# Another order of the seven products of a down projection, other places for the weight sums, and two PSUM tiles for the last two token tiles

## The chip, the cores and the metric

The kernel runs on one core of a Trainium2 chip. The metric is the device time of one execution in microseconds (us); several runs are timed and their median is given. The profile shows one execution, recorded by the hardware profiler. TensorE (PE in the profile) multiplies matrices into PSUM, ScalarE (ACT) and VectorE (DVE) do elementwise work, GpSimd (POOL) here subtracts halves of weights and issues some transfers, SyncE (SP) issues most loads.

## The reference, cut to what matters

One layer of a streaming encoder on 512 tokens and 16 learned meta tokens, d_model 1024, everything in float32. Two mixers (stick-breaking attention and gated linear attention) are merged by gates, projected, normalised and added to the residual. Then the gated MLP follows, with a causal depthwise convolution over tokens, d_ff 2816:

```python
hn = _rmsnorm(h, norm_ffn_pre[l])
up = hn @ w_ffn_up[l]
act = jax.nn.gelu(_causal_dwconv(up, conv_w[l], conv_b[l]), approximate=True)
ffn = (act * (hn @ w_ffn_gate[l])) @ w_ffn_down[l]
h = h + _rmsnorm(ffn, norm_ffn_post[l])
```

The change lies in `@ w_ffn_down` and in the normalisation of its result.

## The kernel before

**Precision.** Every float32 factor is split into a high part, rounded to the format fp32r that TensorE takes (`act.copy`, line 135), and a low part, the difference (`dve.tensor_tensor` subtract, line 136). A product is three matmuls: high by high, high by low, low by high. `split` (lines 134 to 136) does it with one instruction on ScalarE and one on VectorE.

**The down projection by seven products.** The activation A (tokens by d_ff) is cut into 2 x 2 blocks, two halves of the tokens by two halves of d_ff, and so is the weight B (d_ff by d_model). A scheme of the Strassen and Winograd kind computes the four result blocks with seven block products in place of eight. The sums of A blocks (S1 to S4) are made on VectorE at the end of the up/gate loop (lines 963 to 968); those of B blocks are made in place in one buffer `tw`, which first holds B11:

- t1: `tw += B12` (loaded into a small buffer, `raw_t`),
- t2: `tw += B22` (which lies in `tv`),
- t4: `tw += B21` (loaded into `raw_t`), with its signs arranged in the A sums.

`add` (line 1035) issues one such sum on VectorE (line 1039). The buffer `tv` first holds B22; an accumulating transfer issued by GpSimd (`by_transfer`, line 1046) then adds B12 onto it.

The products, with their A operand, B operand and PSUM accumulator: p1 (A11, B11, qa), p5 (S1, tw after t1, qd), p6 (S2, tw after t2, qb), p3 (S4, tv, qd), p7 (S3, tv after the transfer, qb), p4 (A22, tw after t4, qe), p2 (A12, B21 loaded again, qa). The profile names the accumulators dA, dD, dB, dE. p3 adds to what p5 left in qd, p7 to what p6 left in qb, p2 to what p1 left in qa. In between, p1's, p5's and p6's values are read out: a copy of qa on ScalarE (line 1076), a copy of qd on ScalarE (line 1084) and an addition from qb on VectorE (line 1089).

**Chunks.** `product` (lines 996 to 1019) walks d_ff in six chunks (`CH`, line 977: five of two slices of 128, one of one). A chunk splits its weight rows into `wh` and `wl` (128 x 1024), gets the A operand, and gives 12 matmuls of 512 columns (6 in the last). A11 and S1 are split beforehand (`whole`); for the other five products `late_split` (line 1024) splits the A chunk here, into `sh` and `sl` (128 x 512). The last two chunks are issued together, sorted by token tile (line 1015), so the first token tile is complete half of 18 matmuls before the second. `beside` is called once per chunk, after its splits: that is where the sums are put.

**Buffers.** `wh` and `wl` have two buffers in each of two pools, used two chunks in turn; `sh` and `sl` have two; `raw` has three. `tv` lies in the place of A11 and `hbr` (the residual, read back for the end) in the place of S1, so their loads wait for p1's and p5's matmuls. PSUM has eight banks of 128 x 512 float32: `mmt` (line 68) gives a tile of two banks, `pst` (line 71) a tile of one; two of each tag ("mm", "s", "z") exist. Line 1048's `halves` cuts a two-bank tile into its two token tiles.

**What sets the order.** The text of the kernel gives dependencies and priorities: the framework simulates the engines with its own costs when it builds the program, and puts on each engine, at each moment, the earliest-written instruction that is ready in the simulation. An instruction that is written late can so come early. On the chip each engine then keeps this fixed order, and waits where an input is late. Matmuls are ordered in the same way.

**The end.** For each of four token tiles of 128 rows, `square` sums squares on ScalarE (line 1052), `gain` multiplies by the norm's gain on VectorE (line 1055), `finish` (line 1057) forms the reciprocal root from the sums (line 1060 and lines 119 to 131), scales and adds the residual (line 1064, two instructions) and issues two output writes (line 1065). The first two token tiles end with p2.

## Time and profile before

| | |
|---|---|
| median of three runs | 975.08 us (972.68 to 976.45) |
| the profiled execution's own time | 973.69 us |
| its span (first to last instruction) | 972.0 us |
| mean granted TensorE clock | 0.987 |
| TensorE matmul busy | 941.1 us, 97% |
| VectorE busy | 661.6 us, 68% |
| ScalarE busy | 488.8 us, 50% |
| first and last matmul of the down projection start | 851.72 and 961.84 us |

Rows of groups give line, engine, operation, output and inputs with shapes, count, busy time and mean duration. Rows of a timeline give start, duration, engine, line and operation, and in brackets the idle time of the engine before it and what ended that. Where several instructions are merged (x2), the duration runs from the first start to the last end; neighbouring instructions of an engine can overlap a little. A row of windows gives the stretch, its length, then the busy time and count for PE, PEld (weight loads), DVE, ACT and POOL, the granted clock, the DMA engines' share and GB/s.

### The profile page before, as it was taken

Reading aid. Unit: us, or ns where it says so; the run is one execution under the profiler, and the core shown is the slowest. Engines: PE = TensorE matmul, PEld = TensorE weight load, DVE = VectorE, ACT = ScalarE, POOL = GpSimd, SP = SyncE. Lnnn points to the kernel's source line nnn. Section 1 sums busy time; section 2 is a strip of 40 time slices with the busy share of each in tenths; the row PEclk is TensorE's granted clock in tenths of the full one; section 3 lists DMA queues with packets and bytes.
Section 4 is the critical chain, followed back from the end, with each engine's and each line's share of the span. In section 5 each row is a group of like instructions: output and inputs, shape, how many; then the busy total and the mean of one; then the engine's idle time right before and its main releaser. Section 6 shows DMA issues by size and latency. Waiting matters only on the chain.

```text
span 972.0 us, 16625 instructions
## 1 busy us (share of the span) xinstructions
PE 941.1 (97%) x6588; PEld 867.5 (89%) x6588; DVE 661.6 (68%) x1110; ACT 488.8 (50%) x913; POOL 356.6 (37%) x268
## 2 busy tenths in 40 slices
PE   7999999999999998999999899999999999999995
PEld 7999999999999998999998679999999999887874
DVE  6675867767547877777859968555455445489877
ACT  5664645546367565675754245433333333344663
POOL 6523232222234554444545352444444444100200
PEclk9999999999999999999999899999999999999998
DMA  7122212221222221232213363232333332278712
GB/s 215 45 66 66 66 49 62 66 66 45 66 66 66 84 70 45 65 88 61 71 55 96 118 222 119 68 107 88 99 97 87 89 108 87 87 270 296 159 36 105
DMA packets 129727, 92.79 MB, mean 95 GB/s; under 512 B 4064, under 2 KB 114914, under 8 KB 129650
## 3 DMA queue, kind: packets, MB, share of 16 engines
q1 hardware_dynamic: 126178, 82.55, 28.8%
q10 hardware_dynamic: 1968, 6.29, 1.7%
q0 software_dynamic: 1504, 2.88, 1.6%
q8 instruction: 52, 0.85, 0.4%
q14 instruction: 25, 0.20, 0.1%
HBM read 87.52 MB, written 4.19 MB: 94 GB/s over the span
## 4 chain that ended last, share of the span: by engine, by line
PE 80%; DVE 12%; issue 3%; ACT 2%; POOL 2%; DMA 1%; DVEq 0%; POOLq 0%; ACTq 0%
PE pt_up L110 13%; PE ga L956 13%; PE pt_gr L110 5%; PE pt_gv L110 5%; PE pt_mg L110 4%; PE pt_go L110 4%; PE dA L1018 3%; PE pt_gk L110 2%; PE pt_sv L110 2%; PE pt_ms L110 2%; PE wo L890 2%; PE pt_gq L110 2%; PE dD L1018 2%; PE pt_sk L110 2%; PE dB L1018 2%
## 5 line engine op out<-in xcount | busy, mean ns | idle before, releaser
L90 POOL TENSOR_TENSOR wl_up<-raw_up,wh_up 128x1024 fp32r<-128x1024 f32 x22 | 53.0, 2410 | 67.6 <-ACT wh_up L89 67.6
L90 POOL TENSOR_TENSOR wl_ga<-raw_ga,wh_ga 128x1024 fp32r<-128x1024 f32 x22 | 55.2, 2510 | 56.6 <-ACT wh_ga L89 56.6
L110 PE MATMUL pt_up<-h2l,wh_up 128*128 128x256 f32 (+1 forms) x352 | 73.6, 283 | 0.3 <-DVE h2l L205 0.2
L110 PE MATMUL pt_up<-h2h,wh_up 128*128 128x256 f32 (+1 forms) x352 | 73.6, 283 | 0.2 <-ACT h2h L204 0.2
L110 PE MATMUL pt_up<-h2h,wl_up 128*128 128x256 f32 (+1 forms) x352 | 73.2, 282 | 0.0
L956 PE MATMUL ga<-h2h,wl_ga 128*128 128x512 f32 (+1 forms) x192 | 72.2, 376 | 0.0
L956 PE MATMUL ga<-h2l,wh_ga 128*128 128x512 f32 (+1 forms) x192 | 72.2, 376 | 0.0
L956 PE MATMUL ga<-h2h,wh_ga 128*128 128x512 f32 (+1 forms) x192 | 72.0, 375 | 0.0
L89 ACT CAST wh_up<-raw_up 128x1024 fp32r<-128x1024 f32 x22 | 23.0, 1049 | 85.4 <-PE pt_up L110 76.2
L110 PEld LDWEIGHTS pt_up<-h2h,wh_up 128*128 128x128 f32 x352 | 56.9, 189 | 2.2 <-ACT h2h L204 0.5
L110 PEld LDWEIGHTS pt_up<-h2l,wh_up 128*128 128x128 f32 x352 | 55.5, 189 | 0.7 <-DVE h2l L205 0.7
L110 PEld LDWEIGHTS pt_up<-h2h,wl_up 128*128 128x128 f32 x352 | 55.4, 189 | 0.0
L956 PEld LDWEIGHTS ga<-h2h,wl_ga 128*128 128x128 f32 x192 | 36.2, 189 | 7.0
L947 DVE SCALAR_TENSOR_TENSOR cy<-pt_up,cw,cy 128x511 f32<-128x511 f32 (+1 forms) x22 | 16.4, 745 | 37.7 <-ACT cy L944 37.7
L956 PEld LDWEIGHTS ga<-h2l,wh_ga 128*128 128x128 f32 x192 | 36.2, 188 | 6.2
L956 PEld LDWEIGHTS ga<-h2h,wh_ga 128*128 128x128 f32 x192 | 36.2, 188 | 6.1
L947 DVE SCALAR_TENSOR_TENSOR yp<-pt_up,cw,yp 128x511 f32<-128x511 f32 (+1 forms) x22 | 16.4, 745 | 30.9 <-ACT yp L944 30.9
L89 ACT CAST wh_ga<-raw_ga 128x1024 fp32r<-128x1024 f32 x22 | 23.0, 1048 | 25.2 <-PE ga L956 24.7
L135 ACT CAST sh_p<-As 128x512 fp32r<-128x512 f32 (+1 forms) x30 | 17.4, 583 | 30.7 <-PE dB L1018 11.5
L1046 POOL DMA_DIRECT2D tv<-in_w_ffn_down_dram x6 | 7.1, 1184 | 69.2 <-DVE wl_p L136 69.2
L90 POOL TENSOR_TENSOR wl_gr<-raw_gr,wh_gr 128x1024 fp32r<-128x1024 f32 x8 | 19.0, 2370 | 35.9 <-ACT wh_gr L89 33.1
L90 POOL TENSOR_TENSOR wl_gv<-raw_gv,wh_gv 128x1024 fp32r<-128x1024 f32 x7 | 16.9, 2418 | 38.2 <-ACT wh_gv L89 38.2
(558 smaller groups left out, 3265.6 us busy)
## 6 DMA issues: line engine op xcount, KB each, us to landing
raw_up<-in_w_ffn_up_dram SPq DMA_DIRECT2D x22, 512.0 KB, 3.9
raw_ga<-in_w_ffn_gate_dram SPq DMA_DIRECT2D x22, 512.0 KB, 3.8
raw_t<-in_w_ffn_down_dram SPq DMA_DIRECT2D x10, 512.0 KB, 6.7
raw_gv<-in_w_in_dram SPq DMA_DIRECT2D x8, 512.0 KB, 3.8
raw_gr<-in_w_in_dram SPq DMA_DIRECT2D x8, 512.0 KB, 3.9
raw_mg<-in_w_in_dram SPq DMA_DIRECT2D x8, 512.0 KB, 3.8
raw_go<-in_w_gla_out_dram SPq DMA_DIRECT2D x8, 512.0 KB, 4.1
raw_ms<-in_w_in_dram SPq DMA_DIRECT2D x8, 512.0 KB, 3.9
```

What stands on the lines that cost most here:

```text
L89: act.copy(hi_out, raw)
L90: lo_eng.tensor_tensor(out=lo_out, in0=raw, in1=f32(hi_out), op=ALU.subtract)
L110: pe.matmul(dst, a[:, k, :], b[:, k, lo:hi], start=n == 0, stop=n == len(steps) - 1)
L135: act.copy(hi, src)
L890: pe.matmul(d0[i], m[k][:, t], w, start=k == 0 and q == 0, stop=k == 7 and q == 2)
L947: dve.scalar_tensor_tensor(out=y[:, d:], in0=pt[:, : SEQ - d], scalar=c, in1=y[:, d:], op0=ALU.mult, op1=ALU.add)
L956: pe.matmul(pg_[:, lo:hi], a[:, k, :], b[:, k, lo:hi], start=lo == 0 and k == 0 and q == 0, stop=k == KT - 1 and q == 2, skip_group_check= ...
L1018: pe.matmul(dsts[i], a, b, start=first and k == 0 and edge[0], stop=last and k == NP - 1 and edge[1], skip_group_check=True)
L1046: return lambda n, q, nk: pool.dma_start(out=t[:, q : q + nk, :], in_=block(s, c, q, nk), accum_op=ALU.add)
```

## The change

The products are issued in the order p1, p5, p3, p6, p7, p4, p2, where p6 stood before p3. The t2 sums are no longer the source of p6: three of them are issued beside p5's chunks 3 to 5 and three beside p3's chunks 0 to 2 (`t2(-3)` and `t2(3)`). The t4 sums stand beside p6 and p7 instead of p3 and p7, every second chunk each. The accumulating transfers onto `tv` are issued beside p6's chunks instead of p3's. The addition from qb (old line 1089) moves into the loop behind p6, ahead of the subtraction, the square and the gain that used to follow p3.

The PSUM tiles change places: qa, the accumulator of p1 and p2, becomes two tiles of one bank (dA0 and dA1); qd, which was two such tiles, becomes one tile of two banks (dD). qb stays one tile of two banks. The loads of `tv` are written ahead of the copies of qa.

```diff
-        qa = halves(mmt("dA"))
-        product("p1", whole(A11), lambda q, nk: first.get(q, tw[:, q : q + nk, :]), qa, True, True,
-                lambda n, q, nk: add(plain(0, R, "t1"), "t1", q, nk))
+        def t2(shift):
+            def of(n, q, nk):
+                if 0 <= n + shift < len(CH):
+                    add(kept(tv), "t2", *CH[n + shift])
+            return of
+        def t4(odd):
+            def of(n, q, nk):
+                if n % 2 == odd:
+                    add(plain(1, L, "t4"), "t4", q, nk)
+            return of
+        qa = [pst("dA0"), pst("dA1", "z")]
+        product("p1", whole(A11), lambda q, nk: first.get(q, tw[:, q : q + nk, :]), qa, True, True, t1)
...
-        qd = [pst("dD0"), pst("dD1", "z")]
-        product("p5", whole(S1), kept(tw), qd, True, True)
+        qd = halves(mmt("dD"))
+        product("p5", whole(S1), kept(tw), qd, True, True, t2(-3))
         for i in range(2):
             act.copy(yb[:, 2 + i, R], qd[i])
+        product("p3", late_split(S4), kept(tv), qd, False, True, t2(3))
         qb = halves(mmt("dB"))
-        product("p6", late_split(S2), lambda q, nk: add(kept(tv), "t2", q, nk), qb, True, True)
+        product("p6", late_split(S2), kept(tw), qb, True, True, later(by_transfer(tv, 0, R), t4(0)))
         for i in range(2):
             dve.tensor_tensor(out=yb[:, i, R], in0=qb[i], in1=p1[:, i, :], op=ALU.add)
-        tv_sum = by_transfer(tv, 0, R)
-        product("p3", late_split(S4), kept(tv), qd, False, True, half_t4(0))
-        for i in range(2):
             dve.tensor_tensor(out=yb[:, i, R], in0=qd[i], in1=yb[:, i, R], op=ALU.subtract)
             square(i, yb[:, i, R], 1)
             gain(i, yb[:, i, R], R)
-        tv_sum = lambda n, q, nk: None
-        product("p7", late_split(S3), kept(tv), qb, False, True, half_t4(1))
+        product("p7", late_split(S3), kept(tv), qb, False, True, t4(1))
```

`later` calls its jobs one after the other for a chunk; `t1` is the old sum beside p1 under a name.

## The prediction

> **What bounds the kernel now.** I read the page first, then the stages of the down projection, then its waits, then the timelines of single engines around each gap. The page's first rows:

> ```profile
> span 972.0 us, 16625 instructions
> PE 941.1 (97%) x6588; PEld 867.5 (89%) x6588; DVE 661.6 (68%) x1110; ACT 488.8 (50%) x913; POOL 356.6 (37%) x268
> ```

> TensorE sets the pace, and the diff touches only what follows the first matmul of the down projection:

> ```profile
> 851.72 0.40 PE L1018 MATMUL dA<-wh_p,A 128*128 128x512 f32 x1
> ```

> From 851.72 to the end are 120 us. What can be won there is TensorE's idle time and the stretch behind its last matmul; the matmuls themselves, 462, stay. Three of the stages, and the waits of the second one:

> ```profile
> 882.20:897.70 15.50, 13.78 (x57) 10.07 (x55) 15.50 (x18) 7.70 (x12) 1.11 (x1) 1.00 0.78 268
> 900.40:915.50 15.10, 15.10 (x67) 12.21 (x67) 11.76 (x16) 9.19 (x13) 5.13 (x5) 1.00 1.11 227
> 930.80:946.70 15.90, 15.55 (x68) 12.40 (x68) 14.18 (x20) 10.73 (x17) 0.00 (x0) 1.00 0.15 37
> ...
> PEld dB L1018 <- DVE sl_p L136: 3.4, 4, 1.4
> PE dB L1018 <- DVE sl_p L136: 1.8, 3, 0.9
> ```

> The columns are window, length, then busy time (count) of PE, PEld, DVE, ACT, POOL. The first row is product p6 (into dB): VectorE busy 15.50 of 15.50, and only 57 matmuls, where p3 in the next row has 67 in 15.10 with VectorE at 11.76. TensorE waits there for `sl`, the low half of the split A operand. The gaps one by one (start, duration):

> ```profile
> 888.01 0.40 PE L1018 MATMUL dB<-wl_p,sh_p 128*128 128x512 f32 x1
> 888.84 0.50 PE L1018 MATMUL dB<-wh_p,sl_p 128*128 128x512 f32 x1 [0.43 <-DVE sl_p L136]
> 889.17 0.39 PE L1018 MATMUL dB<-wh_p,sh_p 128*128 128x512 f32 x1
> ...
> 894.34 0.40 PE L1018 MATMUL dB<-wl_p,sh_p 128*128 128x512 f32 x1
> 895.19 0.50 PE L1018 MATMUL dB<-wh_p,sl_p 128*128 128x512 f32 x1 [0.45 <-DVE sl_p L136]
> ...
> 896.46 0.40 PE L1018 MATMUL dB<-wl_p,sh_p 128*128 128x512 f32 x1
> 897.79 0.50 PE L1018 MATMUL dB<-wh_p,sl_p 128*128 128x512 f32 x1 [0.94 <-DVE sl_p L136]
> ...
> 934.26 0.39 PE L1018 MATMUL dE<-wl_p,sh_p 128*128 128x512 f32 x1
> 935.00 0.73 PE L1018 MATMUL dE<-wh_p,sl_p 128*128 128x512 f32 x2 [0.35 <-DVE sl_p L136]
> ```

> Matmuls overlap, so I count from start to start. The undisturbed pace is 0.232 (959.75 to 961.84, below, are nine steps). The steps into the waiting matmuls are 0.83, 0.85 and 1.33, which lose 0.60 + 0.62 + 1.10 = 2.3 us; each restart costs another 0.1 (888.84 to 889.17 is 0.33), four of them in p6, so p6 loses about 2.7 us. At p7 to p4 934.26 to 935.00 loses 0.5 more, 0.6 with its restart. The other products run through. So some 3.5 us lie in the middle, and after the last matmul (ends 962.24) the span runs on for 9.8 us.

> **The change part by part.** (1) The t2 sums (tw += tv) leave p6, whose source they were, and stand in p5 and p3, three each; the t4 sums (tw += raw_t) must now follow p6's own splits of tw, so they move from p3/p7 to p6/p7. Where did they run before?

> ```profile
> 892.18 2.35 DVE L1039 TENSOR_TENSOR tw<-tw,raw_t 128x1024 f32<-128x1024 f32 x2
> 896.19 1.22 DVE L1039 TENSOR_TENSOR tw<-tw,raw_t 128x1024 f32<-128x1024 f32 x1
> L1039 DVE TENSOR_TENSOR tw<-tw,raw_t x12: 683/1218/1224, 858.2 to 897.7; 128x1024 f32<-128x1024 f32 x10, 128x512 f32<-128x512 f32 x2
> L1039 DVE TENSOR_TENSOR tw<-tw,tv x6: 684/1218/1226, 875.5 to 885.2; 128x1024 f32<-128x1024 f32 x5, 128x512 f32<-128x512 f32 x1
> ```

> Though written into p3 and p7, the last t4 sum ran at 897.7, still inside p6: the scheduler pulls a sum forward as soon as its inputs allow. The 896.19 one directly holds up the `sl` that ends the 1.33 step. Pitch of such an operation is 2.35 - 1.22 = 1.13, so six sums (five whole, one half) are 6.3 us. After the change p6 holds four of its own weight splits that buffers do not let run earlier (3 x 1.13 + 0.6 = 4.0), four `sl` (2.2), two weight splits of p7 (2.3) and five or six t4 sums (5.7 to 6.3): 14.2 to 14.8 in 15.3, 93 to 97%. That lies between the 100% that lost 2.7 us and the 78% (11.76 of 15.10) that lost nothing; p4 at 89% lost 0.6. I take 0.8 lost in p6 (bounds 0 and 3.2, the old 2.7 and another 0.5 as in p4): **-1.9**, bounds -2.7 to +0.5. The t2 sums cost nothing: they stay limited by tv's landing (the first at 875.5), and p5 and p3 have the room (11.76 of 15.10). If that cover is gone, each is 1.13. What moves with them on the queues:

> ```profile
> raw_t<-in_w_ffn_down_dram SPq DMA_DIRECT2D x10, 512.0 KB, 6.7
> ...
> DMA to landing us min/median/max: 9.0/10.0/10.7
> ```

> The raw_t loads of t4 keep their order on SyncE (three raw buffers, 6.7 us to landing) and are wanted later than before, so they are there. The six accumulating tv transfers (the second row, L1046, alone on GpSimd's queue) need p3's splits of tv and t2's reads of it; p3 now runs a whole product (15.3) ahead of p6, so they start earlier and their 10 us are over before p7. I book nothing for either; a p7 that waits for a transfer would show at its first chunks.

> (2) Product order p1 p5 p6 p3 p7 p4 p2 becomes p1 p5 p3 p6 p7 p4 p2. Before, p5 and p3 (both into dD) had p6 between them, and p6 and p7 (both into dB) had p3. Now they are neighbours, and each first result must be read out before the next product adds to it. **p5 to p3**: ScalarE copies dD.

> ```profile
> 881.95 0.39 PE L1018 MATMUL dD<-wh_p,S 128*128 128x512 f32 x1
> 882.18 0.40 PE L1018 MATMUL dB<-wh_p,sh_p 128*128 128x512 f32 x1
> ...
> 882.25 1.06 ACT L1084 COPY yb<-dD 128x512 f32<-128x512 f32 x2
> ```

> TensorE went on at 882.18 because p6 followed. Now p5's end (882.34) releases both copies, 1.06, and TensorE resumes at about 882.36 + 1.06 + 0.03 = 883.45 instead of 882.18: **+1.3**. Bounds: 0.1 when each half is guarded alone, 2.3 when a 1.06 cast stands ahead on ScalarE. Other matmuls can't fill it: the buffers of sh and sl (two each) belong to p3's first chunks. **p6 to p7**: VectorE adds p1 to dB (L1089). The nearest rows are the same addition at p7 to p4:

> ```profile
> 930.56 0.40 PE L1018 MATMUL dB<-wh_p,sl_p 128*128 128x512 f32 x1
> 930.80 0.43 PE L1018 MATMUL dE<-wh_p,sh_p 128*128 128x512 f32 x1
> ...
> 931.32 1.28 DVE L1111 TENSOR_TENSOR yb<-dB,p 128x512 f32<-128x512 f32 x2
> ```

> An `sl` stood ahead of it, so the pair ended at 932.60, and a next product into dB would have resumed at 932.65 instead of 930.80: **+1.85**. Bounds 0.2 (halves guarded alone) and 3.0 (one more 1.13 operation ahead). Behind it on VectorE then stand p7's `sl` and the two subtractions L1103; p7 has both its first `sl` buffers filled by then, and I book nothing more.

> [...]

> (3) dA becomes two tiles, dA0 and dA1. p2's last matmuls are sorted by token tile, so tile 0 ends nine matmuls early:

> ```profile
> 959.75 0.39 PE L1018 MATMUL dA<-wh_p,sl_p 128*128 128x512 f32 x1
> ...
> 961.84 0.40 PE L1018 MATMUL dA<-wh_p,sl_p 128*128 128x512 f32 x1
> ...
> 962.27 0.60 ACT L1052 ACTIVATE dj<-dA 128x512 f32<-128x512 f32 x1 [4.02 <-PE dA L1018]
> 963.78 0.60 ACT L1052 ACTIVATE dj<-dA 128x512 f32<-128x512 f32 x1
> ...
> 964.57 1.40 DVE L1064 SCALAR_TENSOR_TENSOR yb<-yb,a_out,hbr 128x512 f32<-128x512 f32 x2
> 965.89 0.68 DVE L1055 TENSOR_TENSOR yb<-dA,g3bc 128x512 f32<-128x512 f32 x1
> 967.25 1.41 DVE L1064 SCALAR_TENSOR_TENSOR yb<-yb,a_out,hbr 128x512 f32<-128x512 f32 x2
> ```

> Tile 0 was complete at 960.14, yet its square began at 962.27, with ScalarE idle for 4.02: the wait goes by the whole tile. With two tiles everything of tile 0 moves up by 2.1, its final pair from about 964.4 to 962.3, ending 963.7. Tile 1's square then starts at 962.27 instead of 963.78, its sum at 963.65 behind that pair, its gain multiply at 963.70 instead of 965.89: 2.2 earlier, and the rest follows at the old distances (965.89 to the end of the last row, 968.66, is 2.77): it ends at 966.5, **-2.1** with a little taken off for the order of the small operations. Bounds: -2.8 (tile 1 runs as undisturbed as tile 0 did, 962.27 to 964.4 + 1.41) and -0.2. The output writes keep their distance.

> This also says that the prices of (2) go by the whole tile, since dD and dB are each one tile of two banks after the change.

> **Sum**: -1.9 + 1.3 + 1.85 - 2.1 = -0.85. The profiled execution took 973.69 (span 972.0 and 1.69 around it) and would take 972.8; the median of the runs, 975.08, is 1.4 above it, so I say 974.2.

> **The rivals.** (A) The halves of dD and dB are guarded bank by bank. Half 0 of a product is complete nine matmuls (2.1 us) before half 1, so its read-out is hidden, and the first matmuls of the next product cover the second: +0.3 in place of 3.15, sum -3.7, time 971.4. Against it stands the 962.27 row; for it only that a half is a bank. 17%. [...]

> (B) Slower: VectorE stays full in p6. If the scheduler pulls all six t4 sums into p6, with more than 15.3 us of work there (a seventh 1.13 operation decides), `sl` comes late as before, p6 keeps its 2.7, and L1089 starts behind a further sum: 3.0. Sum 0 + 1.3 + 3.0 - 2.1 = +2.2, time 977.3. For it: the 892.18 and 896.19 rows. Against: t2 is gone from there. 17%.

> (C) The split of dA buys little, because the scheduler places tile 0's last matmul next to tile 1's. It has done so where the tiles are separate already:

> ```profile
> 946.20 0.62 PE L1018 MATMUL dE<-wh_p,sl_p 128*128 128x512 f32 x2
> ...
> 946.63 1.29 DVE L1122 TENSOR_TENSOR yb<-dE,yb 128x512 f32<-128x512 f32 x2
> ```

> Two `sl` matmuls end p4 together and both tiles are read after 946.6. In p2 the 959.75 row stands in its sorted place, which speaks against it. Then -0.3 in (3): sum +0.95, time 976.0. 11%.

> **How the numbers follow.** Forecast 55%, A 17%, B 17%, C 11%. A measurement of this kernel tells 0.5% (4.9 us) from no change: under 970.2 is faster, over 980.0 slower. A crosses that only with (1) near its end of -2.7 and (3) near -2.8, a third of its chance, and scatter adds a little: 7%. B crosses with p6 at 3.2 and both read-outs at their upper ends, a quarter: with scatter 6%. The rest, 87%, is no difference. The range, 971.0 to 977.9, takes in A's and B's values and leaves out their far ends, about 2 in 10. The forecast's own range is 972.4 to 976.2.

> **What would show it.** In the changed profile: p6's `sl` waits of TensorE below 1 us in total (step 1; above 2 us is B); a TensorE wait for ScalarE's copies of dD at the start of p3 and one for VectorE's additions from dB at the start of p7, 1.3 and 1.85 (none is A); a square of dA0 starting about 2.1 us ahead of the last matmul's end, and 7.7 instead of 9.8 us from there to the end of the span (step 3; C if not). The prediction is wrong if the end of the last matmul moves by more than 3 us either way, or if an earlier product gets a stall that it did not have.

## The result, and the profile after

| | before | after |
|---|---|---|
| median, us | 974.42 (971.74 to 976.69, six runs) | 981.19 (979.11 to 982.05, six runs) |
| ratio to before | | 1.0065 (95%: 1.0043 to 1.0088) |
| the profiled execution's own time, us | 973.69 | 982.05 |
| its span, us | 972.0 | 980.3 |
| first start to last end of the down projection's matmuls, us | 851.72 to 962.24 | 852.50 to 971.13 |
| from there to the end of the span, us | 9.8 | 9.2 |

The change made the kernel slower by 0.65%, where 974.2 and "no difference" had been forecast. The profiled execution of after is the slowest of its six. The page of after begins:

```profile
span 980.3 us, 16625 instructions
PE 944.9 (96%) x6588; PEld 871.2 (89%) x6588; DVE 662.2 (68%) x1110; ACT 488.7 (50%) x913; POOL 357.1 (36%) x268
```

The work is the same, and so is every engine's busy time, but for 3.8 us more on TensorE (941.1 before). Some 2.9 of them lie in the two half-clock stretches below (an estimate: 6.76 us of busy time for 17 matmuls that take 3.9 at the pace of 0.23). The down projection's matmuls take 118.6 us instead of 110.5, 8.1 more; another 0.8 lies ahead of them, where the diff touches nothing, and the stretch behind them is 0.6 shorter. The chain of waits of after (start, duration, what) shows the places:

```profile
882.46 0.70 ACT wh_p L135
...
883.42 1.07 ACT yb L1105 x2
...
897.08 8.30 DMA raw_t<-in_w_ffn_down_dram
...
921.56 1.29 DVE yb L1113 x2
```

Three links that are not TensorE's account for what is new: the copies of dD (p5 to p3), a load of 8.30 us in the middle of p6, and the additions from dB (p6 to p7). The second was in no part of the forecast. TensorE's timeline of after at the three places:

```profile
882.72 0.39 PE L1018 MATMUL dD<-wh_p,S 128*128 128x512 f32 x1
884.53 0.50 PE L1018 MATMUL dD<-wh_p,sh_p 128*128 128x512 f32 x1 [1.43 <-ACT yb L1105]
...
903.23 0.39 PE L1018 MATMUL dB<-wl_p,sh_p 128*128 128x512 f32 x1
907.36 0.79 PE L1018 MATMUL dB<-wh_p,sl_p 128*128 128x512 f32 x1 [3.74 <-DVE sl_p L136]
...
920.78 0.39 PE L1018 MATMUL dB<-wh_p,sl_p 128*128 128x512 f32 x1
922.99 0.47 PE L1018 MATMUL dB<-wh_p,sh_p 128*128 128x512 f32 x1 [1.83 <-DVE yb L1113]
...
924.92 0.63 PE L1018 MATMUL dB<-wl_p,sh_p 128*128 128x512 f32 x1
925.35 0.63 PE L1018 MATMUL dB<-wh_p,sl_p 128*128 128x512 f32 x1
```

Counted from start to start against a pace of 0.23, the three steps are 1.81, 4.13 and 2.21 us and lose 1.6, 3.9 and 2.0. Behind the last two the matmuls do not go on at 0.23 but at 0.43 (924.92 to 925.35). The windows of after (window, length, then busy time and count of PE, PEld, DVE, ACT and POOL, the granted clock, the DMA share, GB/s) say why:

```profile
907.30:910.71 3.41, 3.35 (x8) 2.68 (x9) 3.41 (x5) 0.00 (x0) 0.00 (x0) 0.50 0.73 190
924.40:927.81 3.41, 3.41 (x9) 2.69 (x9) 3.35 (x6) 1.61 (x4) 0.00 (x0) 0.50 0.00 0
927.60:939.80 12.20, 12.20 (x54) 9.82 (x53) 7.40 (x10) 6.28 (x11) 0.00 (x0) 0.99 0.01 1
```

The granted clock is 0.50 for 3.41 us behind each of the two gaps, and only 8 or 9 matmuls pass there; later it is 0.99. Each such stretch costs some 1.5 us, an estimate (3.41 us less 8 or 9 steps of 0.23 is 1.6 or 1.3).

Why did the load come so late? VectorE's queue in p6, the transfers that GpSimd issued just before, and the loads of the t4 sums on SyncE's queue, all of after:

```profile
895.82 1.23 DVE L1039 TENSOR_TENSOR tw<-tw,raw_t 128x1024 f32<-128x1024 f32 x1
...
900.77 1.23 DVE L136 TENSOR_TENSOR wl_p<-tw,wh_p 128x1024 fp32r<-128x1024 f32 x1 [0.26 <-ACT wh_p L135]
905.47 1.23 DVE L1039 TENSOR_TENSOR tw<-tw,raw_t 128x1024 f32<-128x1024 f32 x1 [3.48 <-DMA raw_t<-in_w_ffn_down_dram]
906.62 0.69 DVE L136 TENSOR_TENSOR sl_p<-As,sh_p 128x512 fp32r<-128x512 f32 x1
```

```profile
880.66 1.36 POOL L1046 DMA_DIRECT2D tv<-in_w_ffn_down_dram  x1 [47.13 <-DVE wl_p L136]
...
892.46 0.89 POOL L1046 DMA_DIRECT2D tv<-in_w_ffn_down_dram  x1 [0.72 <-DVE wl_p L136]
...
DMA to landing us min/median/max: 7.9/12.0/14.1
```

```profile
874.29 1.58 SPq L991 DMA_DIRECT2D raw_t<-in_w_ffn_down_dram  x2
...
897.08 11.73 SPq L991 DMA_DIRECT2D raw_t<-in_w_ffn_down_dram  x3
```

The t4 sums of chunks 0, 2 and 4 are written beside p6, those of 1, 3 and 5 beside p7. There are three raw buffers, and the loads are issued in written order, so the even chunks' rows lie there early and chunk 1's load is the fourth. It waits for a free buffer, that is for the first sum (895.82), and is issued at 897.08. But the scheduler pulled chunk 1's sum forward, from beside p7 to the second place, into p6, in front of the `sl` that p6's chunk 1 needs (chunks count from 0). On the chip VectorE stood 3.48 us at that sum, and TensorE behind it for the `sl` at 906.62. The load took 8.30 us, while the accumulating transfers, issued from 880.66 to 892.46 with up to 14.1 us to landing, were under way. The mean busy share of the DMA engines from 897.08 to 905.47 was 1.04 (it adds up packets' times; over 1, they overlapped).

At the end, TensorE's and ScalarE's timelines of after:

```profile
970.50 0.63 PE L1018 MATMUL dA<-wh_p,sl_p 128*128 128x512 f32 x2
```

```profile
970.93 0.60 ACT L1052 ACTIVATE dj<-dA 128x512 f32<-128x512 f32 x1 [3.79 <-PE dA L1018]
...
971.65 0.60 ACT L1052 ACTIVATE dj<-dA 128x512 f32<-128x512 f32 x1
```

Two `sl` matmuls, one of each token tile, are the last two of the product. So tile 0's square starts at 970.93, when all but the very last matmul are done, and 0.6 us of the tail are gained instead of 2.1.

### The profile page after: what moved, and what is told of

Read it like the earlier page. It is cut to its first block, busy times and chain, and to the rows that moved or that the text cites. A ratio compares the mean times of both kernels' runs of the same rounds, so it can differ in the third digit from the quotient of the medians.

```text
span 980.3 us, 16625 instructions
## 1 busy us (share of the span) xinstructions
PE 944.9 (96%) x6588; PEld 871.2 (89%) x6588; DVE 662.2 (68%) x1110; ACT 488.7 (50%) x913; POOL 357.1 (36%) x268
## 4 chain that ended last, share of the span: by engine, by line
PE 82%; DVE 10%; issue 3%; ACT 2%; POOL 2%; DMA 1%; DVEq 0%; POOLq 0%; ACTq 0%
PE pt_up L110 13%; PE ga L956 12%; PE pt_gr L110 5%; PE pt_gv L110 5%; PE pt_go L110 4%; PE pt_mg L110 4%; PE dA L1018 3%; PE dB L1018 3%; PE pt_gk L110 2%; PE pt_sv L110 2%; PE dD L1018 2%; PE wo L890 2%; PE pt_ms L110 2%; PE pt_gq L110 2%; PE pt_sk L110 2%
## 5 line engine op out<-in xcount | busy, mean ns | idle before, releaser
L110 PE MATMUL pt_gv<-hnh,wl_gv 128*128 128x272 f32 (+1 forms) x128 | 27.6, 289 | 0.1
## 6 DMA issues: line engine op xcount, KB each, us to landing
raw_up<-in_w_ffn_up_dram SPq DMA_DIRECT2D x22, 512.0 KB, 3.8
raw_ga<-in_w_ffn_gate_dram SPq DMA_DIRECT2D x22, 512.0 KB, 3.9
raw_t<-in_w_ffn_down_dram SPq DMA_DIRECT2D x10, 512.0 KB, 6.9
raw_gv<-in_w_in_dram SPq DMA_DIRECT2D x8, 512.0 KB, 3.8
raw_gr<-in_w_in_dram SPq DMA_DIRECT2D x8, 512.0 KB, 3.8
raw_mg<-in_w_in_dram SPq DMA_DIRECT2D x8, 512.0 KB, 3.9
raw_go<-in_w_gla_out_dram SPq DMA_DIRECT2D x8, 512.0 KB, 4.2
raw_ms<-in_w_in_dram SPq DMA_DIRECT2D x8, 512.0 KB, 3.9
```

The source lines that it names most:

```text
L110: pe.matmul(dst, a[:, k, :], b[:, k, lo:hi], start=n == 0, stop=n == len(steps) - 1)
```

## The experiments

The kernels ran in two sets, each beside the kernel before on the same chip, whose medians there are 974.13 and 974.20; each kernel ran ten or twelve times, where nothing else is said. The theory: (i) a sum that is pulled ahead of its late load stops p6; (ii) the load is late because the accumulating transfers hold the DMA engines; (iii) reading out a two-bank PSUM tile as a whole costs the stops at p5 to p3 and p6 to p7; (iv) the half-clock stretches follow from the gaps of TensorE ahead of them (steps of 4.13 and 2.21 us); (v) the tail is set by the order of the last matmuls. The chief rival to (i) and (ii) is VectorE with too much to do in p6.

**The odd t4 sums held back.** In after, the three sums written beside p7 may not be issued before p6's last weight split.

```diff
-        dve.tensor_tensor(out=lo, in0=src, in1=f32(hi), op=ALU.subtract)
+        split.last = dve.tensor_tensor(out=lo, in0=src, in1=f32(hi), op=ALU.subtract)
...
-        product("p7", late_split(S3), kept(tv), qb, False, True, t4(1))
+        p6_end = split.last
+        def t4_held(n, q, nk):
+            with tc.issue_after(p6_end.ins):
+                t4(1)(n, q, nk)
+        product("p7", late_split(S3), kept(tv), qb, False, True, t4_held)
```

> The changed kernel with one edit: the three t4 sums that its text puts beside p7 are kept behind the last VectorE split of p6. Theory (a sum of p7, pulled forward, stands in front of p6's third sl and waits 3.5 us for its raw_t load): that wait is gone, TensorE loses at most 1.5 us in p6 where it lost 4.1 plus a restart, no matmul of p6 runs at 0.43 us pace, and the gap p6 to p7 grows by at most 1 us because three sums (2.9 us) now stand there. Time 976 to 978 against 981.2. Rival (VectorE has too many sums beside p6, whichever come): p6 keeps more than 2.5 us of loss, time 979 or more.

Measured: 976.26, ratio 1.0020 (1.0006 to 1.0034), span 973.7, as forecast. The gap in p6 is gone (all of p6 loses 0.3). VectorE's and TensorE's timelines at the next place:

```profile
910.54 2.96 DVE L1039 TENSOR_TENSOR tw<-tw,raw_t 128x1024 f32<-128x1024 f32 x3
...
915.15 1.28 DVE L1113 TENSOR_TENSOR yb<-dB,p 128x512 f32<-128x512 f32 x2
```

```profile
913.67 0.39 PE L1018 MATMUL dB<-wh_p,sl_p 128*128 128x512 f32 x1
916.58 0.76 PE L1018 MATMUL dB<-wh_p,sh_p 128*128 128x512 f32 x1 [2.52 <-DVE yb L1113]
```

The three held sums now stand ahead of the additions from dB, with one weight split and one `sl` between, and the step from p6 to p7 grows from 2.21 to 2.91, with 3.41 us of half clock behind it (from 916.22). Even so the ratio to before falls from 1.0065 to 1.0020, some 4.4 us. By itself this does not rule out a full VectorE, since the three sums now run behind p6's last `sl` (910.20). Against it stands that in after VectorE was idle for 3.48 us at the gap and busy for only 15.18 of p6's 20.80 us; the next kernel, with all these sums in the order of after, decides.

**Without the accumulating transfers.** This kernel leaves out the six transfers that add B12 onto `tv`, so that p7 multiplies by B22 alone.

```diff
-        product("p6", late_split(S2), kept(tw), qb, True, True, later(by_transfer(tv, 0, R), t4(0)))
+        product("p6", late_split(S2), kept(tw), qb, True, True, t4(0))
```

> The changed kernel without the six accumulating transfers onto tv (B12 is not added, so p7 multiplies by B22 alone). Theory (the raw_t load of the fourth t4 sum is slow, 8.3 us, because those transfers hold the DMA engines): it lands in 3.5 to 5.5 us after its issue, VectorE does not wait for it by more than 1 us, and TensorE's 4.1 us gap in p6 is gone. Rival (it is late only because its buffer comes free late): landing still takes 8 us or VectorE still waits 3 us.

Measured: 973.41 in one run, span 971.6. The loads' issue on SyncE, and the sum that follows the fourth load on VectorE:

```profile
894.48 9.43 SPq L991 DMA_DIRECT2D raw_t<-in_w_ffn_down_dram  x3
```

```profile
898.31 1.23 DVE L1039 TENSOR_TENSOR tw<-tw,raw_t 128x1024 f32<-128x1024 f32 x1 [0.39 <-DMA raw_t<-in_w_ffn_down_dram]
```

The load is issued at 894.48 and its sum starts at 898.31: at most 3.83 us instead of 8.30, and VectorE waits 0.39 instead of 3.48, though the sum stands one weight split earlier in VectorE's queue than in after. The DMA engines' share in the fortieth of the span that holds the load is 6 tenths (874.4 to 898.7), and in after 9 tenths (882.3 to 906.8). So (ii) holds. All of p6 loses 1.3 us instead of 5.8 with the same sum pulled ahead, so a full VectorE can account for 1.3 at most.

**PSUM pairs.** The kernel with held sums, and in addition qd and qb as two one-bank tiles each; qa and qe pay for it with a two-bank tile.

```diff
-        qa = [pst("dA0"), pst("dA1", "z")]
+        qa = halves(mmt("dA"))
...
-        qd = halves(mmt("dD"))
+        qd = [pst("dD0"), pst("dD1", "z")]
...
-        qb = halves(mmt("dB"))
+        qb = [pst("dB0"), pst("dB1", "z")]
...
-        qe = [pst("dE0"), pst("dE1", "z")]
+        qe = halves(mmt("dE"))
```

> The kernel of e1 with the PSUM tiles changed back for the read-outs: qd and qb are each two tiles of one bank, qa and qe each one tile of two banks. Theory (a read-out waits for, and holds, the whole tile): from p5 to p3 TensorE steps 0.7 us or less into its first matmul where it stepped 1.8, from p6 to p7 1.2 or less where it stepped 2.2; 1.5 to 2.5 us faster than e1. Rival (the copy and the addition are late because ScalarE and VectorE are busy then): the two steps keep over 1.5 us each and the time equals e1 within 0.5 us.

Measured: 974.26, ratio 1.0001 (0.9987 to 1.0015), span 972.6. TensorE's timeline:

```profile
883.01 0.50 PE L1018 MATMUL dD<-wh_p,sh_p 128*128 128x512 f32 x1 [0.49 <-ACT yb L1105]
...
915.62 0.47 PE L1018 MATMUL dB<-wh_p,sh_p 128*128 128x512 f32 x1 [1.92 <-DVE yb L1113]
```

ScalarE's copies at the first of these places:

```profile
882.39 1.06 ACT L1105 COPY yb<-dD 128x512 f32<-128x512 f32 x2
```

At p5 to p3 the wait falls from 1.43 to 0.49, in line with (iii): the two copies run until 883.45, and TensorE goes on at 883.01, so with tiles of one bank the first half's matmuls need only the first half's copy. The step is 0.87, still over the forecast 0.7. At p6 to p7 the forecast of 1.2 or less for the step was missed: 2.31. The held sums still stood ahead of the additions (the pair began at 914.79, p6's last matmuls at 913.31). What is left there is put down to VectorE's queue and not to the tile, which the next kernel tests. The time is 2.0 us under the last kernel's, as forecast, but partly by luck: that kernel lost some 1.5 us to the half clock behind this step (an estimate: 3.05 us of busy time there for 7 matmuls, which take 1.6 at the pace of 0.23), and this one has a granted clock of 1.00 there.

**The same pairs, the sums held one step longer.** The odd sums now follow the second addition from dB instead of p6's last weight split.

```diff
-            dve.tensor_tensor(out=yb[:, i, R], in0=qb[i], in1=p1[:, i, :], op=ALU.add)
+            p6_end = dve.tensor_tensor(out=yb[:, i, R], in0=qb[i], in1=p1[:, i, :], op=ALU.add)
...
-        p6_end = split.last
```

> The kernel of e3 with its three held t4 sums moved from in front of the additions from dB to behind the second of them. Theory (in e3 the 2.3 us step from p6 to p7 was the queue on VectorE, the tiles alone would make it small): the step falls under 1 us, and the time is 1 to 2 us under e3's 974.3 unless p7 loses it again. Rival (the addition must wait for p6's last matmul even with a tile for each half): the step stays above 1.5 us.

Measured: 974.39, ratio 1.0007 (0.9993 to 1.0020), span 972.3. TensorE's timeline:

```profile
911.76 0.47 PE L1018 MATMUL dB<-wh_p,sh_p 128*128 128x512 f32 x1 [0.65 <-ACT sh_p L135]
...
917.47 0.85 PE L1018 MATMUL dB<-wh_p,sl_p 128*128 128x512 f32 x2 [1.75 <-DVE sl_p L136]
```

The wait for the additions is gone (what ends the step is an `sh`), though the step of 1.04 is just over the forecast of less than 1. But on VectorE the sums that were moved behind the additions now stand ahead of the `sl` of p7's chunk 1:

```profile
914.40 1.82 DVE L1039 TENSOR_TENSOR tw<-tw,raw_t 128x1024 f32<-128x1024 f32 x2
...
916.74 0.68 DVE L136 TENSOR_TENSOR sl_p<-As,sh_p 128x512 fp32r<-128x512 f32 x1
```

That is a step of 2.14 with 3.41 us of half clock behind it. The stall moved with the sums into p7, which the forecast had left open, and the time stayed where it was.

**Fillers between p6 and p7.** After, with eight extra matmuls behind p6 into dE0, which p4 later starts afresh, so their result is never read.

```diff
+        qe = [pst("dE0"), pst("dE1", "z")]
+        fa, fb, fm = last_mm2
+        with tc.issue_after(fm.ins):
+            for _ in range(8):
+                pe.matmul(qe[0], fa, fb, start=True, stop=True, skip_group_check=True)
         product("p7", late_split(S3), kept(tv), qb, False, True, t4(1))
```

> The changed kernel with eight matmuls of 512 columns more, into the still unused dE0, queued on TensorE between p6 and p7, where it waits 2.2 us for the additions from dB; their result is overwritten. Theory (the half pace behind p7's start follows from the idle stretch): p7 starts when it did, within 0.3 us of the same distance from p6's last matmul, and no matmul of p7 runs at 0.43 us pace, which saves 1.5 us in p7. Rival (the half pace has another cause, such as the load on PSUM or the amount of work in a stretch of time): eight matmuls of p7 still run at 0.43.

Measured: 977.87 in one run, span 975.8. Windows behind p6's gap and behind the fillers:

```profile
904.50:907.91 3.41, 3.41 (x9) 2.67 (x10) 3.41 (x4) 0.00 (x0) 0.00 (x0) 0.50 0.79 205
```

```profile
920.00:923.40 3.40, 3.39 (x16) 2.75 (x16) 3.40 (x5) 2.23 (x4) 0.00 (x0) 1.00 0.00 0
```

The gap in p6, left as it was, still has its half clock. Where TensorE was kept busy with useless work, the step from p6's last matmul to p7's first is 2.21 us as in after, yet p7 starts at a granted clock of 1.00. So the second stretch is caused by TensorE's idling, not by the place in the program or by what p7 does. This is (iv). It was not spared by where the gap falls in the clock's grid (see the last section): without the fillers 1.82 us of idling (918.22 to 920.04) would lie in one stretch of the grid (918.15 to 921.57, four times 3.413 behind the half clock's start at 904.50), as in after. One run's time proves little; the trace carries this.

**The split of dA alone.** The kernel before, with only the PSUM tiles changed as in after.

```diff
-        qa = halves(mmt("dA"))
+        qa = [pst("dA0"), pst("dA1", "z")]
...
-        qd = [pst("dD0"), pst("dD1", "z")]
+        qd = halves(mmt("dD"))
```

> The kernel before with the PSUM part of the change alone: dA is two tiles of one bank, dD one tile of two banks; order of the products and sums as before. Theory (the scheduler puts the last matmul of token tile 0 next to that of tile 1 once they are separate): the first square of dA starts less than 0.5 us before the last matmul ends, the span after the last matmul shrinks by 0.3 to 0.8 us from 9.8, no new gap in p5, and the time is that of before within 1 us. Rival (the loss of the tail's gain comes from the later state of the engines in the changed kernel): the square starts 2.1 us before the last matmul's end and the tail shrinks by 2 us.

Measured: 974.93, ratio 1.0007 (0.9995 to 1.0019), span 972.4: nothing gained. TensorE's last entry and ScalarE's first square:

```profile
962.61 0.63 PE L1018 MATMUL dA<-wh_p,sl_p 128*128 128x512 f32 x2
```

```profile
963.04 0.60 ACT L1052 ACTIVATE dj<-dA 128x512 f32<-128x512 f32 x1 [3.79 <-PE dA L1018]
```

As in after, one `sl` matmul of each tile stands at the very end. The tail is 9.2 us instead of 9.8, but the down projection's matmuls take 111.7 instead of 110.5, so that gain is lost again.

**The split, with the order held.** The same kernel, and p2's last 18 matmuls kept in the written order, one issued after the other.

```diff
-                    pe.matmul(dsts[i], a, b, start=first and k == 0 and edge[0], stop=last and k == NP - 1 and edge[1], skip_group_check=True)
+                    with tc.issue_after(kept_mm[0].ins) if kept_mm[0] and nm == "p2" and n == len(CH) - 1 else ExitStack():
+                        kept_mm[0] = pe.matmul(dsts[i], a, b, start=first and k == 0 and edge[0], stop=last and k == NP - 1 and edge[1], skip_group_check=True)
```

> The kernel of e5 with the last 18 matmuls of p2 held in their written order on TensorE, token tile 0 first. Theory: the first square starts about 2.1 us before the last matmul's end, and the span after it is 7.5 to 8.0 us where it was 9.8: 1.5 to 2.3 us faster than e5. Rival (the end is set by tile 1's own chain and the output writes): within 0.5 us of e5.

Measured: 972.39, ratio 0.9993 (0.9975 to 1.0010), span 969.8. TensorE and ScalarE at the end:

```profile
961.81 0.40 PE L1020 MATMUL dA<-wh_p,sl_p 128*128 128x512 f32 x1
```

```profile
960.14 0.60 ACT L1054 ACTIVATE dj<-dA 128x512 f32<-128x512 f32 x1 [1.92 <-PE dA L1020]
```

Tile 0's square starts 2.1 us before the last matmul ends (962.21), and the tail is 7.6 us instead of 9.2. The trace shows these 1.6 us; the two ratios' intervals overlap, so the times alone do not prove them (one of this kernel's ten runs took 978.36).

**The old order, with the sums spread by hand.** On top of the last kernel, the six t4 sums are given places in p3 (chunks 0, 1, 3) and p7 (chunks 2, 3, 5); all but the one at p3's chunk 0 are held behind that chunk's splits.

```diff
-                if n % 2 == o:
-                    add(plain(1, L, "t4"), "t4", q, nk)
+                if n in places:
+                    with tc.issue_after(split.last.ins) if n else ExitStack():
+                        add(plain(1, L, "t4"), "t4", *CH[places[n]])
...
-        product("p3", late_split(S4), kept(tv), qd, False, True, half_t4(0))
+        product("p3", late_split(S4), kept(tv), qd, False, True, t4_at({0: 0, 1: 1, 3: 2}))
...
-        product("p7", late_split(S3), kept(tv), qb, False, True, half_t4(1))
+        product("p7", late_split(S3), kept(tv), qb, False, True, t4_at({2: 3, 3: 4, 5: 5}))
```

> The kernel of e6, which keeps the old order of the products, with the six t4 sums placed by hand: the first free, the second and third behind the splits of p3's chunks 1 and 3, the others behind those of p7's chunks 2, 3 and 5. Theory (p6's gaps came from VectorE's sums in front of sl): p6 loses under 1 us where it lost 2.7, no product gains a gap of over 0.5, and the time is 3 to 4.5 us under before, 969.5 to 971. Rival (the sums only carry the gaps to p3 and p7, or p6's gaps come from t2): 1 to 2 us under before, as e6.

Measured: 970.49, ratio 0.9959 (0.9947 to 0.9972), span 968.7. This beats both kernels, the one before by 0.4%. The only wait of TensorE that its timeline shows in p6, p3 and p7:

```profile
888.64 0.50 PE L1020 MATMUL dB<-wh_p,sl_p 128*128 128x512 f32 x1 [0.99 <-DVE sl_p L136]
```

p6 loses 1.3 us where before lost 2.7; less than 1 was forecast. In the traces that is the gain on the last kernel (span 968.7 against 969.8); against before, 2.2 of the 3.3 us are the tail (7.6 instead of 9.8). In VectorE's queue the last t2 sum (885.03) and two weight splits stand ahead of the `sl` that ends this wait (887.90); whether the t2 sums can be placed better was not tried.

## Why the prediction was wrong

By the medians the forecast missed by 7.0 us (974.2 and 981.19). In the profiled execution's own terms the forecast was a span of 971.15 (972.0 - 0.85), and 980.3 was measured, 9.2 more. The terms, with losses counted from start to start as in the prediction:

| step | forecast, us | measured, us | more than forecast |
|---|---|---|---|
| (1) p6 loses | 0.8 | 5.8, of it 3.9 + 0.4 gap and restart, 1.3 half clock | 5.0 |
| (2) p5 to p3 | 1.3 | 1.7 with the restart | 0.4 |
| (2) p6 to p7 | 1.85 | 2.06 with the restart | 0.2 |
| half clock behind p6 to p7 | no term | 1.55 | 1.55 |
| (3) the tail | -2.1 | -0.6 | 1.5 |
| start of the down projection | 0 | 0.8 | 0.8 |

They add up to 9.45; the 0.3 too much are small steps of before that after no longer has. The last row is not the change's: the kernels are the same up to that point, and their first t1 sum, which starts 6.5 us behind it in before and after, starts at 856.4 in the kernel without transfers, at 858.1 in that with the split alone, at 858.2 in before and at 859.0 in after.

**Step (1) failed**, and with it the forecast, in this sentence: "The raw_t loads of t4 keep their order on SyncE (three raw buffers, 6.7 us to landing) and are wanted later than before, so they are there." The prediction had itself shown that the scheduler pulls sums forward across products (the 892.18 and 896.19 rows), and used that to count five or six of them in p6. It did not ask which one comes when. Loads go in written order, and the odd sums' loads come behind the even ones', while VectorE's order came out otherwise: the sum that depends on the fourth load went second. The two orders cross, and the price is the whole wait of a load that could only be issued 0.03 us after the first sum ended.

**In the same step the transfers were booked at nothing**, because "their 10 us are over before p7". They were; the harm was not to p7 but to the load beside them: 8.30 us with them, at most 3.83 without.

The working on VectorE's share (93 to 97% of p6) was about the wrong quantity. Rival (B) had p6 keep its 2.7 us by a full VectorE; p6 did worse than that while VectorE stood still (busy 15.18 of 20.80 us, 73%), and with the same sums but without the transfers it lost 1.3.

**Step (2) was right in kind and nearly in size.** The whole two-bank tile guards the read-out, as the 962.27 row had said, and rival (A) is out: 1.7 and 2.06 against 0.3 for both. The 0.4 over at p5 to p3 is a cast of 0.70 on the path that stood ahead of the copies (882.46 in the chain), the case named as its upper bound. What step (2) lacked is the half clock behind a gap. In the down projection of before the granted clock is 1.00 throughout (851.72 to 962.24, longest step 1.33), but the trace of before has such stretches further ahead, behind the mean granted clock of 0.987: from 374.20 to 377.61 TensorE is busy for 1.14 of 3.41 us, and from 377.61 to 381.02 the granted clock is 0.50. That half clock can follow such idling (2.27 us) could have been read there.

**Step (3) was rival (C)**, 11% in the forecast: -0.6 by the trace against the -0.3 given there. The tile-wise wait was read rightly, and the 2.1 us were there to be had once the order was held (the kernel with p2's order held). What failed was "the 959.75 row stands in its sorted place, which speaks against it". That row was placed while dA was one tile; with the PSUM tiles changed and nothing else the sorted order was lost, as the kernel with the split alone shows.

The forecast's own criteria did point there: the last matmul's end moved by more than 3 us (8.9), and p6's `sl` waits are above 2.

## What to carry to other kernels

When a scheduler may reorder instructions, compare two orders before booking a prefetch at nothing: that in which an engine consumes, and that in which the loads are issued into a few rotating buffers; where they crossed here, VectorE waited 3.48 us for a load and TensorE 3.74 for the `sl` queued behind it. A second transfer queue that starts earlier was not free either (8.30 us for that load, at most 3.83 without it): look up which loads will land beside it. And a gap of TensorE of two microseconds should be priced with what the clock may take afterwards, which here was up to three quarters as much again (1.55 us behind a loss of 2.06).

## What the hardware showed unexpectedly

```profile
920.99:924.40 3.41, 1.58 (x7) 1.22 (x7) 3.41 (x5) 2.34 (x3) 0.00 (x0) 1.00 0.00 0
```

```profile
914.52:917.93 3.41, 1.66 (x8) 1.05 (x7) 3.41 (x5) 2.29 (x4) 0.00 (x0) 1.00 0.63 202
917.93:921.34 3.41, 3.41 (x10) 2.63 (x9) 3.41 (x5) 1.57 (x4) 0.00 (x0) 0.50 0.70 254
```

```profile
914.05:917.46 3.41, 1.84 (x8) 1.56 (x9) 3.41 (x6) 1.14 (x2) 0.00 (x0) 1.00 0.96 314
917.46:920.87 3.41, 3.41 (x17) 2.73 (x16) 3.41 (x6) 1.95 (x3) 0.00 (x0) 1.00 0.10 39
```

```profile
911.25:914.66 3.41, 2.82 (x12) 1.80 (x10) 2.15 (x4) 1.48 (x3) 0.00 (x0) 1.00 0.69 225
914.66:918.07 3.41, 2.20 (x10) 1.83 (x11) 3.41 (x6) 2.13 (x5) 0.00 (x0) 1.00 0.00 0
918.07:921.48 3.41, 3.41 (x16) 2.77 (x15) 3.41 (x5) 2.34 (x6) 0.00 (x0) 1.00 0.00 0
```

Idle times of 1.83 (3.41 - 1.58) and 1.75 were followed by a cell at half clock, 1.57 was not. They are counted by the profile's matmul records, whose ends are modelled. The kernel without transfers has nearly the same step from p6 to p7 as after (2.20), but it fell across two cells, 0.59 and 1.21 idle, and the granted clock stayed at 1.00. So in these runs gaps of about 2 us were followed by a loss of some 1.5 us or by none, and what differs between them is how they fell in the grid. Idle time in the cell before does not give a rule: earlier in the trace of after a cell with 1.74 us idle (579.65 to 583.06) was followed by a clock of 1.00 and one with 1.71 (545.52 to 548.93) by 0.50, in before one with 1.13 (268.38 to 271.80) by 0.50 as well, and in after one in which TensorE was busy for all of its 3.41 us, with 32 matmuls (589.89 to 593.30), also by 0.50. That idling counts was tested directly only by the fillers; what else counts stays open.
